# A new table of delays between the interleaved instruction streams of a hybrid decoder layer

## The chip, the cores and the metric

The kernel runs on one core of one Trainium2 chip. The metric is the time of one launch in microseconds (us). Three runs of the kernel before took 1193.43, 1197.82 and 1200.17 us, median 1197.82.

## The reference, cut to what matters

One decoder layer is applied to a prompt of 512 tokens (with 16 learned meta tokens in front) and to 8 samples of 8 new tokens each, with a cache of 2048 keys and values per sample in pages of 128.

```python
xn = rmsnorm(x, p['ln_mix_pre'])
h = xn @ p['w_in']                       # one projection for everything below
da_q, da_k, da_v, gdn_qkv, gdn_z, gdn_b, gdn_a, gate_a, gate_b = jnp.split(h, SPLIT_POINTS, axis=-1)
o_a = attn_fn(q, k, v, lam)              # differential attention: prompt (causal) or sample (paged cache)
o_a = (rmsnorm(o_a, p['da_subln']) * (1.0 - lam_init)).reshape(bsz, t, DA_V_WIDTH)
qkv, new_gdn_conv = causal_dwconv(gdn_qkv, gdn_conv_buf, p['gdn_conv_w'])
# gated DeltaNet (GDN), 4 heads: a triangular solve per chunk, then a recurrence over chunks
o_b = rmsnorm(o_b, p['gdn_norm']) * jax.nn.silu(gdn_z...)
mix = jax.nn.sigmoid(gate_a) * (o_a @ p['w_branch_a']) + jax.nn.sigmoid(gate_b) * (o_b @ p['w_branch_b'])
x = x + rmsnorm(mix @ p['w_out'], p['ln_mix_post'])
# then a gated feed-forward block with a causal convolution of width 3
up, gate = jnp.split(xn @ p['w_ffn_in'], 2, axis=-1)
x = x + rmsnorm((jax.nn.gelu(gate) * up) @ p['w_down'], p['ln_ffn_post'])
```

The outputs are the two groups' rows and the new keys, values and states.

## The kernel before, in words

Activations stand transposed, with channels on the 128 partitions and the 592 tokens (512 prompt, 64 sample, 16 meta) along the free axis. A dense product is made in two halves of the token axis, 256 and 336 columns (or 322, where most meta tokens are not needed). Each operand is split into a rounded part and a remainder (`split`), and a product is three matmuls for each 128 channels: high by high, high by low, low by high. Half a product over 1024 channels is thus a group of 24 matmuls (`dense_steps`).

The stages follow each other: embedding and queries; then a part in which two streams of work are merged; then the rest of the mix, the output projection and the feed-forward block. The change acts on the merged part alone.

The two streams are Python generators. `main` is the prompt's attention (`da_main`: a stream that makes keys and values and projects GDN head 0, merged with one that uses them, head by head), then the four GDN heads (`gdn`: the chain of one head merged with the projection and convolution of the next), then the split of the GDN output. `rest` is the sample attention in chunks of 256 keys (`sample_attention`: four pairs of samples, each of eight chunks and one for the new keys), then the sixteen products for the gates (`gate`), and then the first branch product (`branch_a`), which waits until `spare` is set, when the base inversion of the last GDN head has been emitted.

A chain of GDN (`gdn_chain`) is a row of dependent steps: decays, transposed and normalised keys, the Gram matrices, the inverse of 16x16 diagonal blocks by 14 steps on VectorE (`gdn_base`), larger blocks by TensorE (`gdn_solve`), the samples' states, then four chunks of the recurrence, then the z gate. Between steps it yields a delay out of the table, `yield DELAY[n]`: entries 1 to 5 lie before the base inversion, 12 right after it, 13 to 17 in the solve (15 is used twice), 6 to 8 in the samples' states, 9 to 11 in the recurrence, four times each. Entry 0 ends a projection. Entries 21 to 25 lie in the keys, the meta attention and the prompt attention (23 after the norm of a head's output, 24 after a block's softmax, 25 after the transposition of its weights). Entry 26 lies in each chunk of the sample attention, between the transposition of the weights and their product with the values; the loads of the chunk's value pages are emitted before it, and the next chunk's keys too.

The planner, `merge`, keeps a clock: `work`, the planned time of all matmuls emitted so far, plus `idle`. Each stream has a share, and of those that are ready the one furthest behind its share emits up to its next yield. A stream that yields a delay isn't ready until the clock has moved on by so much:

```python
n = math.prod(rhs.shape[1:])
self.work += (1.68e-3 if lhsT.dtype == F32 and lhsT.shape[1] > 32 else 0.42e-3) * n
...
if s[3] > self.work + self.idle + 1e-6:
    continue
...
s[3] = self.work + self.idle + delay
```

A transposition counts as 0.11 us. When nobody is ready, `drain` moves the clock by 0.1 us of `idle` and asks again. While the prompt attention runs, `main` has share 600 (`MAIN_1`) and `rest` has `REST_W`; in the GDN heads `main` has 1e9, so that `rest` emits only while `main` waits. A planned half group costs 24 x 256 x 0.42e-3 = 2.58 or 24 x 336 x 0.42e-3 = 3.39 us; the gates yield twice as often (steps of 1.29 and 1.62 us).

What the planner makes is the order of emission. The framework then orders each engine's instructions, taking that order for priorities, and gives out buffers: the pages of the cache have six buffers (`page`, line 1386 loads them), transposed keys four, TensorE's results in PSUM two for `d` (dense products), three for `t`, two for `g` and one for `s`. The gates' buffers take the memory of the sample attention, so that the gates' tanh (line 1587) can't run before that attention has ended. All loads are issued by SyncE's queue.

Lines that the prediction speaks of: 275 is every matmul, 423 every transposition, 317 and 318 the two parts of a split; 656 a convolution's multiply-add; 798 and 799 scale the keys; 1352 normalises attention rows; 1469 is the exponential of a chunk of the sample attention; 1587 a gate's tanh; 1603 the branch product's evacuation.

Of the kernel before, what the change touches and what calls it, by code (L numbers as in the profile page):

```python
# [52 lines left out]
def _lay_out_constants():  # L53
# [76 lines left out]


DELAY = (
    10.08, 5.4, 0.6, 0.6, 6.0, 1.3, 0.9, 0.85, 1.32, 1.0, 1.68, 0.17, 26.0, 0.67, 2.93, 0.77,
    0.09, 0.85, 0.38, 2.28, 0.05, 1.54, 0.74, 1.56, 6.12, 0.84, 1.4, 11.52, 1.4, 1.68, 10.28,
)
KEYS = 2
CHUNKS_S = PAST // 256
# [8 lines left out]
FINE = 8  # L146
MAIN_1 = 600.0
MAIN_2 = 1e9
REST_W = 165.0


class Body:
# [39 lines left out]
    def run(self):  # L192
# [14 lines left out]
        with ExitStack() as sm:  # L207
            with ExitStack() as s1:
# [3 lines left out]
                with ExitStack() as s2:  # L212
# [17 lines left out]
                    def main():  # L230
                        head = {}
                        yield from self.da_main(dpool, self.gdn_project(0, head))
                        da.close()
                        self.chain = True
                        self.psum_g = self.pool(ctx, "psum_g", space=PSUM)
                        with ExitStack() as s:
                            self.gpool = self.pool(s, "gpool")
                            yield from self.gdn(head)
                        yield from self.mix_parts(self.pool(s2, "mix"))

                    def rest():
                        with ExitStack() as s:
                            yield from self.sample_attention(self.pool(s, "sa", side="right"))
                        self.gates, self.gtpool = {}, self.pool(sm, "gates", side="right")
                        for i in range(16):
                            yield from self.gate(i)
                        while not self.spare:
                            yield None
                        yield from self.branch_a()

                    self.drain(self.merge((main(), lambda: MAIN_2 if self.chain else MAIN_1), (rest(), REST_W)))
                    self.banks = "ggsttdd"
# [2047 lines left out]
```

## Time and profile before

| what | us |
|---|---|
| median of the runs | 1197.82 |
| lowest and highest run | 1193.43, 1200.17 |
| the profiled execution's own time | 1194.08 |
| its span, from first to last instruction | 1192.2 |
| TensorE matmul busy | 1133.1 |
| VectorE busy | 741.1 |
| ScalarE busy | 554.9 |
| mean granted TensorE clock | 0.985 |

A profile is one execution. Busy time is a union over an engine's instructions; PE stands for matmuls, PEld for loads of weights beside them, DVE for VectorE, ACT for ScalarE, POOL for GpSimd, SP for SyncE, and a trailing q for an engine's instruction queue. A row of a line gives the shortest, median and longest duration in ns, and the first and the last start in us. In a table by stretches each engine has its busy us and, in brackets, its number of instructions. In a row of waits stand the us in total, the number of waits and the longest.

### The profile page before, as it was taken

What the parts mean: (1) busy time and instruction counts of PE and PEld (TensorE: products, weight loads), DVE (VectorE), ACT (ScalarE), POOL (GpSimd) and SP (SyncE); (2) the same over time, 40 slices, a digit from 0 to 9 for tenths busy, and PEclk for the clock granted to TensorE, in tenths of its full rate; (3) what the DMA queues carried; (4) which work ended last, traced back from release to release, by engine and by line L of the source; (5) the groups of instructions that cost most, each with busy time, mean ns of one, the idle gap of its engine ahead of it and who ended that gap; (6) DMA issues with size and microseconds to landing.
All of it is one profiled execution on the core that took longest, in us unless ns stands there. A gap on an engine that the chain in (4) does not pass through costs nothing. (4 is left out here: it accounts for less than half of the span.)

```text
span 1192.2 us, 23895 instructions
## 1 busy us (share of the span) xinstructions
PE 1133.1 (95%) x8683; PEld 1019.3 (85%) x8683; DVE 741.1 (62%) x2007; ACT 554.9 (47%) x1421; POOL 223.5 (19%) x348
## 2 busy tenths in 40 slices
PE   6999999989988999999998999999999999999997
PEld 5987788777657767999988787789999999999996
DVE  5447667785448535763357585479899889842323
ACT  5235444554554553433332445355555555732321
POOL 2122221130001001100010001334554544300000
PEclk9999999999999989999999999999999999999999
DMA  6357454648685863232311245233333322432322
GB/s 201 79 206 224 153 159 132 202 127 307 220 279 188 295 201 92 73 90 56 105 56 45 65 124 177 96 107 106 99 91 91 106 85 86 131 102 79 97 74 80
DMA packets 184349, 157.57 MB, mean 132 GB/s; under 512 B 12570, under 2 KB 146273, under 8 KB 184231
## 3 DMA queue, kind: packets, MB, share of 16 engines
q1 hardware_dynamic: 179713, 147.53, 40.5%
q0 software_dynamic: 3264, 5.16, 1.2%
q10 hardware_dynamic: 1254, 3.35, 0.9%
q8 instruction: 69, 1.13, 0.4%
q14 instruction: 49, 0.40, 0.1%
HBM read 146.12 MB, written 9.88 MB: 131 GB/s over the span
## 5 line engine op out<-in xcount | busy, mean ns | idle before, releaser
L318 DVE TENSOR_TENSOR wlo<-wraw,whi 128x512 fp32r<-128x512 f32 x196 | 138.4, 720 | 139.1 <-ACT whi L317 138.0
L275 PE MATMUL ps_d<-xhi,whi 128*128 128x256 f32 (+2 forms) x704 | 218.9, 311 | 0.0
L275 PE MATMUL ps_d<-xhi,wlo 128*128 128x256 f32 (+2 forms) x704 | 214.2, 305 | 1.3 <-DVE wlo L318 1.3
L275 PE MATMUL ps_d<-xlo,whi 128*128 128x256 f32 (+2 forms) x704 | 214.2, 304 | 0.3 <-DVE xlo L318 0.2
L317 ACT CAST whi<-wraw 128x512 fp32r<-128x512 f32 (+1 forms) x198 | 117.4, 610 | 176.4 <-PE ps_d L275 88.9
L275 PEld LDWEIGHTS ps_d<-xhi,whi 128*128 128x128 f32 x704 | 135.2, 192 | 5.1 <-issue 3.1
L275 PEld LDWEIGHTS ps_d<-xlo,whi 128*128 128x128 f32 x704 | 135.2, 192 | 3.9 <-issue 2.6
L275 PEld LDWEIGHTS ps_d<-xhi,wlo 128*128 128x128 f32 x704 | 134.8, 192 | 4.0 <-DVE wlo L318 2.0
L1421 ACT COPY KT<-ps_t 128x512 f32<-128x512 f32 x107 | 59.1, 588 | 41.6 <-PE ps_t L423 41.4
L423 PE MATMUL ps_t<-consts,page 128*128 128x128 f32 x512 | 73.6, 286 | 2.7 <-DVE o L1480 2.6
L423 PEld LDWEIGHTS ps_t<-consts,page 128*128 128x128 f32 x512 | 60.0, 147 | 15.9 <-PE ps_t L275 5.7
L275 PE MATMUL ps_t<-fhit,hw 128*128 128x290 f32 x228 | 68.0, 298 | 0.0
L275 PE MATMUL ps_t<-flot,hw 128*128 128x290 f32 x228 | 67.7, 297 | 0.0
L275 PE MATMUL ps_t<-fhit,lw 128*128 128x290 f32 x228 | 67.6, 297 | 0.0
L317 ACT CAST hw<-sw 128x512 fp32r<-128x512 f32 x76 | 47.2, 622 | 41.4 <-PE ps_g L275 20.1
L318 DVE TENSOR_TENSOR lw<-sw,hw 128x512 fp32r<-128x512 f32 x76 | 60.2, 792 | 6.4 <-ACT hw L317 6.3
L275 PE MATMUL ps_s<-KT,qb 128*32 128x256 f32 x512 | 44.0, 392 | 3.3 <-DVE xc L974 1.8
L275 PEld LDWEIGHTS ps_t<-flot,hw 128*128 128x128 f32 x228 | 43.3, 190 | 0.0
L275 PEld LDWEIGHTS ps_t<-fhit,lw 128*128 128x128 f32 x228 | 43.1, 189 | 0.0
L275 PEld LDWEIGHTS ps_t<-fhit,hw 128*128 128x128 f32 x228 | 43.0, 189 | 0.0
L275 PE MATMUL ps_t<-page,pT 128*32 128x256 f32 x512 | 38.5, 410 | 0.9 <-ACT pT L1432 0.9
L1978 DVE SCALAR_TENSOR_TENSOR fy<-fpre,fw,fy 128x592 f32<-128x592 f32 x44 | 36.5, 831 | 1.0 <-ACT fy L1976 0.2
(700 smaller groups left out, 3076.7 us busy)
## 6 DMA issues: line engine op xcount, KB each, us to landing
page<-in_cache_k SPq DMA_DIRECT2D x128, 256.0 KB, 3.3
page<-in_cache_v SPq DMA_DIRECT2D x128, 256.0 KB, 4.5
wraw<-in_w_in SPq DMA_DIRECT2D x88, 256.0 KB, 3.3
wraw<-in_w_ffn_in SPq DMA_DIRECT2D x50, 256.0 KB, 3.2
wraw<-in_w_down SPq DMA_DIRECT2D x40, 256.0 KB, 3.1
raw<-in_w_ffn_in SPq DMA_DIRECT2D x38, 256.0 KB, 2.8
wraw<-in_w_out SPq DMA_DIRECT2D x16, 256.0 KB, 2.9
x<-in_x_prompt SPq DMA_DIRECT2D x4, 512.0 KB, 8.8
```

Source lines behind the costliest of these rows:

```text
L275: return self.nc.tensor.matmul(out, lhsT, rhs, **kw).ins
L317: self.nc.scalar.copy(hi, raw)
L318: (eng or self.nc.vector).tensor_tensor(out=lo, in0=raw, in1=hi.bitcast(F32), op=ALU.subtract)
L423: self.nc.tensor.transpose(out, in_, self.ident[:k, :k])
L1421: copy(kt[:, :, 128 * j : 128 * j + 128], tp)
L1978: nc.vector.scalar_tensor_tensor(out=y, in0=pre[:, j : j + 592], scalar=fw[:, m, 16 + j : 17 + j], in1=y, op0=ALU.mult, op1=ALU.add)
```

## The change

24 of the 31 entries of the table of delays get new values, and the share of the second stream goes from 165.0 to 168.5. The code that uses them is untouched.

```diff
 DELAY = (
-    10.08, 5.4, 0.6, 0.6, 6.0, 1.3, 0.9, 0.85, 1.32, 1.0, 1.68, 0.17, 26.0, 0.67, 2.93, 0.77,
-    0.09, 0.85, 0.38, 2.28, 0.05, 1.54, 0.74, 1.56, 6.12, 0.84, 1.4, 11.52, 1.4, 1.68, 10.28,
+    9.27, 2.17, 0.6, 0.6, 1.61, 1.42, 3.06, 2.05, 0.23, 1.0, 3.15, 0.12, 25.87, 1.27, 2.93, 1.46,
+    0.06, 0.16, 0.13, 2.31, 0.54, 1.29, 0.49, 6.72, 6.58, 0.14, 3.65, 11.52, 1.4, 1.3, 10.28,
 )
...
-REST_W = 165.0
+REST_W = 168.5
```

Entry by entry, old to new: 0: 10.08 to 9.27; 1: 5.4 to 2.17; 4: 6.0 to 1.61; 5: 1.3 to 1.42; 6: 0.9 to 3.06; 7: 0.85 to 2.05; 8: 1.32 to 0.23; 10: 1.68 to 3.15; 11: 0.17 to 0.12; 12: 26.0 to 25.87; 13: 0.67 to 1.27; 15: 0.77 to 1.46; 16: 0.09 to 0.06; 17: 0.85 to 0.16; 18, 19 and 20: 0.38, 2.28, 0.05 to 0.13, 2.31, 0.54; 21: 1.54 to 1.29; 22: 0.74 to 0.49; 23: 1.56 to 6.72; 24: 6.12 to 6.58; 25: 0.84 to 0.14; 26: 1.4 to 3.65; 29: 1.68 to 1.3.

## The prediction

> **What bounds the kernel now.** I read the page first (span, engines, slices), then busy time by stage, then the stretches in which TensorE stood idle.
>
> ```profile
> span 1192.2 us, 23895 instructions
> PE 1133.1 (95%) x8683; PEld 1019.3 (85%) x8683; DVE 741.1 (62%) x2007; ACT 554.9 (47%) x1421; POOL 223.5 (19%) x348
> PEclk9999999999999989999999999999999999999999
> ```
>
> TensorE is busy for 95% of the span, so work is conserved and only the other 59 us, and time at a lower granted clock, can be won. The change can act only while the streams are merged. The stage table gives that part (columns: stretch in us, its length, busy us and instruction count of PE, PEld, DVE, ACT, POOL, then granted clock, DMA share, GB/s):
>
> ```profile
> 52.00:240.00 188.00, 183.17 (x1495) 151.58 (x1495) 120.16 (x468) 89.15 (x268) 43.29 (x87) 0.99 0.55 172
> 240.00:357.00 117.00, 106.47 (x1006) 79.90 (x1005) 67.42 (x254) 64.61 (x191) 12.78 (x22) 0.97 0.72 235
> 357.00:460.00 103.00, 94.78 (x850) 72.63 (x850) 59.78 (x218) 51.34 (x159) 8.55 (x20) 0.93 0.67 219
> 460.00:618.00 158.00, 156.88 (x1173) 152.55 (x1173) 81.68 (x233) 59.08 (x169) 11.68 (x18) 1.00 0.28 74
> 618.00:690.00 72.00, 64.33 (x435) 57.27 (x434) 48.48 (x153) 23.40 (x69) 5.02 (x5) 0.95 0.18 53
> ```
>
> The stretches are prompt attention (52 to 240) and then the four GDN heads. Idle PE is length less busy: 4.8, 10.5, 8.2, 1.1 and 7.7 us, together 32.3. Clock lost is length times (1 - clock): 3.5 us in the first head, 7.2 in the second, 3.6 in the last. What sets the stretches apart is the filler beside the chain. The rows of the sample attention's exponential (by source line, asked for each head), of the gates' tanh and of the branch product show which filler ran when (the last two numbers of each are first and last start):
>
> ```profile
> L1469 ACT ACTIVATE S<-S,nm x14: 342/509/513, 264.3 to 353.9; 128x256 f32<-128x256 f32 x13, 128x64 f32<-128x64 f32 x1
> L1469 ACT ACTIVATE S<-S,nm x11: 337/509/513, 386.4 to 449.5; 128x256 f32<-128x256 f32 x9, 128x64 f32<-128x64 f32 x2
> L1587 ACT ACTIVATE gt<-ps_d x32: 380/409/457, 459.9 to 618.2; 128x256 f32<-128x256 f32 x16, 128x322 f32<-128x322 f32 x16
> L1603 DVE SCALAR_TENSOR_TENSOR gt<-gt,ps_d x16: 410/450/492, 631.4 to 669.0; 128x256 f32<-128x256 f32 x8, 128x322 f32<-128x322 f32 x8
> ```
>
> So heads 0 and 1 are filled with 14 and 11 chunks of sample attention, head 2 with gates, head 3 with the branch product alone. Beside gates PE idles 1.1 us in 158; beside chunks 18.7 in 220. Per chunk the loss is (18.7 + 3.5 + 7.2) / 25 = 1.2 us. And between the last gate (618.2) and the first branch product (631.4) filler is missing, which the timeline of PE shows (start, length, what, idle before it and its releaser):
>
> ```profile
> 620.11 0.39 PE L275 MATMUL ps_d<-vt,whi 128*128 128x256 f32 x1 [0.60 <-DVE vt L318]
> ...
> 622.67 0.26 PE L423 MATMUL ps_t<-consts,kn 80*128 80x80 f32 x1 [1.35 <-DVE kn L798]
> ...
> 627.89 0.53 PE L275 MATMUL ps_d<-q,whi 128*128 128x256 f32 x2 [0.62 <-ACT q L317]
> ...
> 630.60 0.57 PE L275 MATMUL ps_d<-qb,whi 128*128 128x256 f32 x1 [2.18 <-DVE qb L318]
> ```
>
> One more reading decides how much a delay can do. The gates' tanh starts at 459.9, yet matmuls of the first gate (322 columns; the z gate has that width too, but its first half is evacuated only at 469.5, first row) lie among the chunks of head 1:
>
> ```profile
> L714 ACT ACTIVATE z<-ps_d x2: 385/410/436, 469.5 to 474.8; 128x256 f32<-128x256 f32 x1, 128x322 f32<-128x322 f32 x1
> ...
> 407.93 0.39 PE L275 MATMUL ps_d<-xhi,wlo 128*128 128x322 f32 x1
> 408.16 0.31 PE L275 MATMUL ps_d<-xhi,whi 128*128 128x322 f32 x1
> ...
> 412.19 0.60 PE L423 MATMUL ps_t<-consts,page 128*128 128x128 f32 x4
> 412.54 0.39 PE L275 MATMUL ps_d<-xhi,whi 128*128 128x322 f32 x1
> ```
>
> The code emits a half group in one piece, and page transposes stand inside one here. So the order of emission is a priority and not the order on PE: a step emitted before its inputs are ready doesn't block PE, and one emitted late can still be pulled up. Delays decide who goes first among what is ready. That makes all terms small.
>
> **The change, part by part.** No instruction, DMA or byte is added or removed; the table moves whole steps against each other. Costs come from the profiled execution (1194.1 us, span 1192.2), 3.7 below the median of the runs, 1197.8.
>
> *Entries without effect: 0.* Numbers 18 to 20 and 29 are never reached (the tail solve returns before its first wait; 27 to 30 are not read). Entry 22 is one wait in the meta attention, shorter by 0.25: 0.
>
> *The share of the second stream, 165 to 168.5.* It gets 2% more of about 45 us of planned work up to 240, a quarter of a chunk: 0, because the chunk runs in one place or the other.
>
> *Prompt attention: entries 21, 23, 24, 25.* Entry 23 (after the norm of a head's output, once per head) goes from 1.56 to 6.72, the others by +0.46, -0.70 and -0.25. PE did wait at that spot:
>
> ```profile
> PE ps_t L423 <- DVE on L1352: 3.0, 3, 1.3
> ```
>
> The gain is at most these 3.0 us. The loss: 4 x 5.16 = 21 us of planned waiting, filled by keys, projections and chunks; only the last head has little of them, so one wait, 5 us, bounds it. With PE busy 183.2 of 188 I take -1 (the row of the idle time lies nearer than a bare wait). Ends -3 and +5.
>
> *Head of the GDN chain: entries 1, 4, 5 and 12.* Per head 5.4 + 6.0 + 1.3 + 26.0 = 38.7 becomes 2.17 + 1.61 + 1.42 + 25.87 = 31.1. The chain asks for its steps 7.6 us sooner, and the next head's projection (17.9 planned) is then not wholly in front of the base inversion. VectorE has to do convolution and inversion side by side: it is busy 16.85 of 19 us in 262 to 281 even now. What is late next is the projection's convolution, which only the next head needs. I take 0. The rows for both (that stretch, a convolution's multiply-add by its line, PE's waits for the scaled keys):
>
> ```profile
> 262.00:281.00 19.00, 16.58 (x168) 12.01 (x168) 16.85 (x92) 9.08 (x26) 1.12 (x3) 0.91 0.81 273
> ...
> L656 DVE SCALAR_TENSOR_TENSOR cy<-pre,cw,cy x36: 836/846/862, 185.7 to 504.5; 128x616 f32<-128x616 f32 x36
> ...
> PE ps_t L423 <- DVE kn L798: 2.5, 2, 1.4
> ```
>
> Ends: -4 (the 2.4 us that PE idles in that first stretch and the 1.7 us of clock lost there) and +8 (the three multiply-adds of one convolution, 0.85 us each, in front of the inversion in heads 0 to 2, 7.6 us). What PE waited for the scaled keys, 2.5 us, can grow or shrink within these.
>
> *Solve, tail and recurrence: entries 6, 7, 8, 10, 11, 13, 15, 16, 17.* Solve 9.01 to 10.27 (15 is used twice), tail 3.07 to 5.34, recurrence 4 x 2.85 = 11.4 to 4 x 4.27 = 17.1: together +9.2. Beside gates a delay is rounded up to gate steps of 1.3 or 1.6 planned us; about two more steps per head come out. In heads 1 and 2 PE has work for them. In head 3 filler is short at the end: +1, ends 0 and +4.
>
> *The chunk's own wait: entry 26, 1.4 to 3.65.* A chunk is planned as 16 + 2 transposes of 0.11 and 16 products of 0.107, that is 3.70 us. When nothing else is ready, the planner lets the wait run idle, and this idle time counts against the chain's delays too. A chunk alone then uses up 5.10 us of chain delays before and 7.35 after. With the sums above (chain 63.4 to 65.0 per head, less 17.9 for the projection) chunks per head fall to (47.1 / 7.35) / (45.5 / 5.10) = 0.72 of what they were: from 14 to about 10 in head 0, and some 8 in head 1. Seven chunks are left for head 2, and eight or nine gates (7 x 7.35 / 5.83) move from head 2 to head 3. What this saves:
> - Head 3 has gates beside its beginning, and the branch product is emitted later. The four gaps above (4.8 us) go, and the clock there (3.6 us lost in that stretch) half comes back. Late next is the second of the two, the chain's own 0.7 us steps on VectorE, so I take -5; ends -8 and 0.
> - Heads 0 to 2 have the same 25 chunks over about 45 us more. If the loss per chunk stays 1.2 us, nothing is won; if it goes with density, a quarter of 29 us goes. I take -4; ends -12 and +8 (seven chunks, now in a head where the loss was nearly nil, bring 1.2 us each).
>
> On the clock: a 6.5 us stretch of head 1, PE busy for all but 0.2 us of it and most of that small products and transposes, was granted 0.81.
>
> ```profile
> 415.00:421.50 6.50, 6.33 (x48) 4.25 (x45) 0.49 (x2) 2.10 (x6) 0.00 (x0) 0.81 0.68 245
> ```
>
> The Trainium skill (TensorE: Matmul & The Clock Gate, Part 4) says that transposes do not count as PE activity for the clock gate. The stretch agrees with it; by that rule the clock lost would follow the number of transposes, which stays, and the forecast would be some 2 us higher.
>
> The sum: -1 + 0 + 1 - 5 - 4 = -9 us. On the profiled 1194.1 this gives 1185; on the median of the runs 1189. The forecast is **1188 us**, between the two and nearer to the median.
>
> **Rivals.** About 6 us, 0.5%, is what a measurement of this kernel can tell from no change.
>
> *Nothing to tell.* Order on PE is set by readiness, as the gate matmuls at 408 show, and the two tables then give nearly the same program. Against it: gates did stay out of head 3, and chunks out of head 2. Time 1192 to 1204, centre 1198. Chance 0.20.
>
> *Slower: the chunk's value pages are held longer.* The loads of a chunk's value pages are emitted ahead of the lengthened wait, and the products that free them after it. All pages share six buffers and a chunk takes four, so each chunk may hold up the next one's loads by 3.65 - 1.4 = 2.25 us. For it speaks that the load queue waits just there in heads 0 and 1 (waits of the DMA queue, 240 to 460):
>
> ```profile
> SPq L1386 <- PE ps_t L275: 45.6, 19, 6.4
> SPq L1386 <- PE ps_t L423: 26.3, 24, 11.0
> ...
> page<-in_cache_v SPq DMA_DIRECT2D x128, 256.0 KB, 4.5
> ```
>
> The first row is loads waiting for the value product. Against it: a value page takes 4.5 us from issue to landing (last row, DMA issues), so part of the longer wait has to pass anyway, and PE pulls up other work. If ten of the 25 chunks pay in full, it costs 22.5 us and the sum is +13: 1211. It decides against the forecast from four paying chunks on. Chance 0.30, by itself or with convolution in the way of the inversion.
>
> *Much faster.* Filler lasts to the end of the chain, and the loss per chunk halves: -5 - 12, and 3 more from the stretch to 690: 1178 to 1170, centre 1174. Against it: by my count 88 planned us of delays in head 3 (60 gate steps of 1.46) still meet only 8 or 9 gates and the branch product, about 73. Chance 0.10.
>
> **How the numbers follow.** Forecast (1178 to 1191) 0.40, much faster 0.10, nothing to tell 0.20, slower 0.30. Faster by over 0.5% is the first two, 0.50; the likeliest single case is the forecast, and its own range is 1178 to 1191. The range leaves out the far parts of the outer cases: 1168 to 1214, from the ends of the chunk and head-3 terms below to the priced slower rival above.
>
> **What would show it.** In the profile of the changed kernel: exponentials of chunks still after 460 and the first gate tanh well after 480; the last gate tanh after 640; no PE gap over 1 us between last gate and first branch product; a granted clock in heads 0 and 1 above 0.95. If the loss per chunk is the same, idle time appears beside chunks in head 2 instead. If the value pages are held, the load queue's waits for the value product grow beyond 45.6 us. The prediction is wrong if chunks end at 450 as before (the wait was filled anyhow), or if PE idles beside the inversions with VectorE full.

## The result, and the profile after

| what | before | after |
|---|---|---|
| median of the runs | 1195.81 us (beside the runs of after) | 1156.80 us (1156.19 to 1157.30) |
| ratio, 95% interval | | 0.967 (0.9637 to 0.9702) |
| span of the profiled execution | 1192.2 us | 1154.8 us |

The new table is faster by 3.3%, 39 us, where 10 us were forecast. It lies below the whole range. The direction was right and so was the place, the part where the streams are merged; the size was not.

The page of after (its span, engines, and the clock by slices):

```profile
span 1154.8 us, 23883 instructions
PE 1113.5 (96%) x8683; PEld 1009.6 (87%) x8683; DVE 738.9 (64%) x2007; ACT 553.4 (48%) x1421; POOL 219.6 (19%) x348
PEclk9999999999999999999999999999999999999999
```

The same 8683 matmuls are busy for 20 us less (1133.1 before), and the slice of the clock that stood at 8 is gone. Busy time hides the clock: in these traces products of 256 columns start 120 ns apart at full clock and 213 ns apart at half clock, transposes 109 and 213.

The merged part ends where the rest of the mix begins (the first evacuation of the second branch product), at 689.2 before and at 651.3 after. The next rows give the merged part and what follows, columns as in the stage table of the prediction. Before:

```profile
52.00:689.20 637.20, 604.82 (x4946) 513.13 (x4946) 376.72 (x1321) 287.17 (x852) 81.32 (x150) 0.98 0.49 153
689.20:1192.20 503.00, 486.98 (x3458) 469.04 (x3456) 339.25 (x615) 246.03 (x526) 134.70 (x179) 0.99 0.34 102
```

After:

```profile
52.00:651.30 599.30, 585.30 (x4946) 503.62 (x4946) 373.21 (x1320) 284.72 (x851) 80.16 (x150) 1.00 0.52 162
651.30:1154.80 503.50, 487.08 (x3458) 469.10 (x3457) 340.65 (x617) 246.84 (x527) 131.88 (x179) 0.99 0.35 103
```

The rest is the same, 503.0 and 503.5 us, and the whole gain, 637.2 - 599.3 = 37.9 us, lies in the merged part, with 4946 matmuls in both. It has three parts. Idle PE falls from 637.20 - 604.82 = 32.4 to 14.0 us, by 18.4. Time at half clock falls from nine windows of 3.41 us (30.7 us) to one (3.4 us); by the spacings above nearly half of each is lost, so that is at most 13.7. The other 5.8 us, at least, are busy time at full clock.

Where PE idled: each head has a beginning (from the start of its chain to the end of the base inversion) and a rest. In heads 0 and 1 of before these are the two rests:

```profile
280.00:357.00 77.00, 70.22 (x681) 50.95 (x680) 31.78 (x111) 42.83 (x123) 3.81 (x7) 0.98 0.81 265
402.00:477.00 75.00, 70.85 (x613) 54.40 (x613) 30.76 (x100) 35.63 (x105) 4.20 (x7) 0.93 0.57 189
```

And all eight stretches of after, beginning and rest by turns:

```profile
240.00:275.00 35.00, 33.44 (x304) 26.92 (x302) 31.18 (x136) 19.41 (x59) 7.25 (x15) 1.00 0.63 204
275.00:325.00 50.00, 49.18 (x483) 37.25 (x483) 24.94 (x85) 28.58 (x87) 3.72 (x6) 1.00 0.69 224
325.00:364.00 39.00, 35.59 (x318) 30.95 (x316) 35.49 (x140) 19.85 (x65) 7.05 (x14) 1.00 0.68 221
364.00:419.00 55.00, 53.43 (x521) 40.14 (x521) 27.03 (x89) 31.69 (x95) 3.21 (x6) 1.00 0.72 235
419.00:461.00 42.00, 39.63 (x343) 33.68 (x343) 36.05 (x140) 21.50 (x69) 6.73 (x11) 1.00 0.70 221
461.00:520.00 59.00, 57.97 (x476) 52.06 (x477) 26.75 (x72) 24.04 (x72) 3.64 (x6) 1.00 0.35 97
520.00:553.00 33.00, 31.36 (x238) 30.56 (x238) 26.44 (x102) 14.13 (x44) 2.90 (x2) 1.00 0.26 63
553.00:647.00 94.00, 94.00 (x718) 92.30 (x718) 35.01 (x75) 29.55 (x74) 2.71 (x3) 1.00 0.27 74
```

The rests of heads 0 and 1 idle 0.8 and 1.6 us instead of 6.8 and 4.2, the last head's rest not at all, and every stretch has the full clock. Over four heads, beginnings idle 9.0 us (14.0 before) and rests 3.4 (13.0 before).

Which filler ran when (rows of the chunks' exponential asked for heads 0, 1 and 2, the gates' tanh, and the first row of the branch product's evacuation):

```profile
L1469 ACT ACTIVATE S<-S,nm x10: 361/509/541, 256.5 to 323.3; 128x256 f32<-128x256 f32 x9, 128x64 f32<-128x64 f32 x1
L1469 ACT ACTIVATE S<-S,nm x10: 348/510/529, 353.3 to 416.4; 128x256 f32<-128x256 f32 x9, 128x64 f32<-128x64 f32 x1
L1469 ACT ACTIVATE S<-S,nm x5: 350/508/512, 451.1 to 470.9; 128x256 f32<-128x256 f32 x4, 128x64 f32<-128x64 f32 x1
L1587 ACT ACTIVATE gt<-ps_d x32: 383/408/448, 482.4 to 610.9; 128x256 f32<-128x256 f32 x16, 128x322 f32<-128x322 f32 x16
L1603 DVE SCALAR_TENSOR_TENSOR gt<-gt,ps_d x20: 412/450/492, 614.2 to 675.0; 128x256 f32<-128x256 f32 x10, 128x322 f32<-128x322 f32 x10
```

Heads 0 to 2 have 10, 10 and 5 chunks where they had 14, 11 and 0. The last chain ends at 647. Of the 20 evacuations in the last row the first 16 belong to the first branch product, and the last of these starts at 650.3: filler lasts to the end. Chains are shorter too; they end at 325, 419, 520 and 647 (357, 477, 608 and 684 before).

### The profile page after: what moved, and what is told of

Its sections match the earlier page's. It is cut to its first block, busy times and chain, and to the rows that moved or that the text cites. A ratio compares the mean times of both kernels' runs of the same rounds, so it can differ in the third digit from the quotient of the medians.

```text
span 1154.8 us, 23883 instructions
## 1 busy us (share of the span) xinstructions
PE 1113.5 (96%) x8683; PEld 1009.6 (87%) x8683; DVE 738.9 (64%) x2007; ACT 553.4 (48%) x1421; POOL 219.6 (19%) x348
## 4 chain that ended last, share of the span: by engine, by line
PE 78%; issue 9%; DVE 6%; ACT 2%; POOL 2%; DMA 1%; SPq 0%; DVEq 0%; POOLq 0%; ACTq 0%
PE ps_d L275 29%; PE ps_t L275 21%; PE ps_g L275 15%; PE ps_t L423 7%; PE ps_s L275 5%; PE ps_m L275 1%; POOL grr L387 1%; ACT KT L1421 1%; DVE cy L656 1%; DVE wlo L318 0%; DVE row L978 0%; DVE xc L980 0%; DMA page<-in_cache_v 0%; DVE row L979 0%; DMA x<-in_x_prompt 0%
## 5 line engine op out<-in xcount | busy, mean ns | idle before, releaser
L423 PE MATMUL ps_t<-consts,page 128*128 128x128 f32 x512 | 69.4, 277 | 0.4 <-ACT KT L1421 0.3
L423 PEld LDWEIGHTS ps_t<-consts,page 128*128 128x128 f32 x512 | 56.9, 141 | 12.7 <-issue 5.1
L275 PE MATMUL ps_t<-page,pT 128*32 128x256 f32 x512 | 36.0, 384 | 0.0
```

The costliest lines, as they stand in the source:

```text
L275: return self.nc.tensor.matmul(out, lhsT, rhs, **kw).ins
L423: self.nc.tensor.transpose(out, in_, self.ident[:k, :k])
```

## Experiments

Each is a change of the order of work alone. Ratios are to the kernel before, run on the same chip beside them. "Chunks" are the numbers of chunks' exponentials in the prompt part (up to 240) and in heads 0, 1, 2; "idle" and "half clock" are PE's idle time and the time at half clock in the merged part.

### Single groups of the table, on the old table

The chunk's wait alone:

```diff
-    0.09, 0.85, 0.38, 2.28, 0.05, 1.54, 0.74, 1.56, 6.12, 0.84, 1.4, 11.52, 1.4, 1.68, 10.28,
+    0.09, 0.85, 0.38, 2.28, 0.05, 1.54, 0.74, 1.56, 6.12, 0.84, 3.65, 11.52, 1.4, 1.68, 10.28,
```

> Entry 26 alone goes from 1.4 to 3.65. Theory A (the filler is spread out: fewer chunks in heads 0 and 1, gates left for head 3) puts most of the gain here: 1160 to 1175, with exponentials of chunks after 460 and gates' tanh up to 600 or later. Theory B (the chain's own delays, entries 1 to 17, now fit its steps) expects 1188 to 1198. Theory C (prompt attention and the second stream's share) expects 1193 to 1198.

Measured: 1171.1 us, ratio 0.9809 (0.9788 to 0.9831), -24 us. Chunks 10, 9, 9, 8; idle 16.4, half clock 6.8 us. So one number carries most of it, as theory A expected. The last chain ends at 635 and filler is left over, which then runs alone:

```profile
635.00:664.00 29.00, 29.00 (x219) 29.00 (x218) 16.79 (x32) 7.19 (x14) 0.00 (x0) 1.00 0.28 83
```

PE isn't idle there, but 29 us of dense products lie behind the chain that could have lain beside it.

The head of the GDN chain (entries 1, 4, 5, 12) alone:

```diff
-    10.08, 5.4, 0.6, 0.6, 6.0, 1.3, 0.9, 0.85, 1.32, 1.0, 1.68, 0.17, 26.0, 0.67, 2.93, 0.77,
+    10.08, 2.17, 0.6, 0.6, 1.61, 1.42, 0.9, 0.85, 1.32, 1.0, 1.68, 0.17, 25.87, 0.67, 2.93, 0.77,
```

> Entries 1, 4, 5 and 12 alone (the chain's steps up to the base inversion asked for 7.6 us sooner per head). Theory A expects 1190 to 1200. Theory B expects 1165 to 1185, with heads that begin their inversion 5 us or more sooner. Theory C expects 1193 to 1198.

Measured: 1188.43, 0.9946 (0.9926 to 0.9966), -6.5 us; chunks 11, 12, 13, 0, idle 32.4, half clock 23.9. None of the three theories gave this time. Idle time is that of before (32.4 us); what fell is the time at half clock, by 6.8 us.

Solve, tail and recurrence (entries 6, 7, 8, 10, 11, 13, 15 to 17) alone:

```diff
-    10.08, 5.4, 0.6, 0.6, 6.0, 1.3, 0.9, 0.85, 1.32, 1.0, 1.68, 0.17, 26.0, 0.67, 2.93, 0.77,
-    0.09, 0.85, 0.38, 2.28, 0.05, 1.54, 0.74, 1.56, 6.12, 0.84, 1.4, 11.52, 1.4, 1.68, 10.28,
+    10.08, 5.4, 0.6, 0.6, 6.0, 1.3, 3.06, 2.05, 0.23, 1.0, 3.15, 0.12, 26.0, 1.27, 2.93, 1.46,
+    0.06, 0.16, 0.38, 2.28, 0.05, 1.54, 0.74, 1.56, 6.12, 0.84, 1.4, 11.52, 1.4, 1.68, 10.28,
```

> Entries 6, 7, 8, 10, 11, 13, 15, 16 and 17 alone (solve, samples' states and recurrence wait 9.2 us longer per head). Theory A expects 1195 to 1205, since chains grow longer and filler runs out sooner. Theory B expects 1175 to 1190. Theory C expects 1193 to 1198.

Measured: 1208.51, 1.0125 (1.0094 to 1.0155), +13.6 us; chunks 11, 16, 9, 0, idle 39.3, half clock 42.9; slower than even theory A expected. Head 0 has 16 chunks instead of 14: longer chain delays beside a short chunk wait crowd them there.

The prompt's entries (0 and 21 to 25, with the share 168.5) alone:

```diff
-    10.08, 5.4, 0.6, 0.6, 6.0, 1.3, 0.9, 0.85, 1.32, 1.0, 1.68, 0.17, 26.0, 0.67, 2.93, 0.77,
-    0.09, 0.85, 0.38, 2.28, 0.05, 1.54, 0.74, 1.56, 6.12, 0.84, 1.4, 11.52, 1.4, 1.68, 10.28,
+    9.27, 5.4, 0.6, 0.6, 6.0, 1.3, 0.9, 0.85, 1.32, 1.0, 1.68, 0.17, 26.0, 0.67, 2.93, 0.77,
+    0.09, 0.85, 0.38, 2.28, 0.05, 1.29, 0.49, 6.72, 6.58, 0.14, 1.4, 11.52, 1.4, 1.68, 10.28,
-REST_W = 165.0
+REST_W = 168.5
```

> Entries 0, 21, 22, 23, 24, 25 and the second stream's share alone on the old table. Taken back from the new table they cost 12.5 us. If they act by themselves: 1180 to 1186. If they act only where the chunks are spread out: 1191 to 1198.

Measured: 1189.55, 0.9963 (0.9936 to 0.9991), -5.3 us, between the two ranges. The four groups alone give -24 - 6.5 + 13.6 - 5.3 = -22; together they give -39.

### Groups taken back from the new table

The chunk's wait taken back to 1.4:

```diff
-    0.06, 0.16, 0.13, 2.31, 0.54, 1.29, 0.49, 6.72, 6.58, 0.14, 3.65, 11.52, 1.4, 1.3, 10.28,
+    0.06, 0.16, 0.13, 2.31, 0.54, 1.29, 0.49, 6.72, 6.58, 0.14, 1.4, 11.52, 1.4, 1.3, 10.28,
```

> The new table with entry 26 back at 1.4. Theory A expects most of the gain gone: 1180 to 1196, gates ended before head 3 begins. Theory B and theory C expect 1157 to 1165.

Measured: 1201.11, 1.0061 (1.0039 to 1.0083). Chunks 12, 15, 9, 0; idle 36.1, half clock 27.3. Without entry 26 all the other edits together make the kernel 0.6% slower, more than theory A expected; in their company it is worth 44 us.

Solve, tail and recurrence taken back:

```diff
-    9.27, 2.17, 0.6, 0.6, 1.61, 1.42, 3.06, 2.05, 0.23, 1.0, 3.15, 0.12, 25.87, 1.27, 2.93, 1.46,
-    0.06, 0.16, 0.13, 2.31, 0.54, 1.29, 0.49, 6.72, 6.58, 0.14, 3.65, 11.52, 1.4, 1.3, 10.28,
+    9.27, 2.17, 0.6, 0.6, 1.61, 1.42, 0.9, 0.85, 1.32, 1.0, 1.68, 0.17, 25.87, 0.67, 2.93, 0.77,
+    0.09, 0.85, 0.13, 2.31, 0.54, 1.29, 0.49, 6.72, 6.58, 0.14, 3.65, 11.52, 1.4, 1.3, 10.28,
```

> The new table with the old values of entries 6, 7, 8, 10, 11, 13, 15, 16 and 17. These cost 13.6 us alone on the old table, since they pack more filler into each head. If they cost the same beside entry 26: 1140 to 1148, faster than the new table. Theory D: they are the counterweight to entry 26 and the time is 1158 to 1170, with filler left over after the last chain as with entry 26 alone.

Measured: 1164.27, 0.9747 (0.9725 to 0.977), 7.5 us above the new table. So this group costs 13.6 us alone and saves 7.5 beside the long chunk wait: its sign depends on entry 26. Without it the last chain ends at 615 and the leftover runs alone for longer:

```profile
615.00:659.00 44.00, 44.00 (x330) 44.00 (x329) 18.60 (x34) 10.46 (x22) 0.00 (x0) 1.00 0.27 77
```

Idle time is as in after (14.2 us), so the loss is mostly busy time at full clock. What makes it is only argued. The chunks' products of 32 columns run four at a time, started 7 ns apart (the 512 with the keys, 382 ns each, are busy for 45.0 us in the page of after). At full clock, two such groups start 196 ns apart; from the last of them to other work it is 310 ns, and the first of them starts some 90 ns late behind other work. So a run broken off by other work costs about 0.2 us. There are 56 unbroken runs of such products in after and 69 here, which would make some 3 us. Over the 20 traces of this case, busy time at full clock goes with the number of runs (correlation 0.8), but before has 56 too and at least 5.8 us more than after, so this isn't all of it.

The prompt's edits taken back:

```diff
-    9.27, 2.17, 0.6, 0.6, 1.61, 1.42, 3.06, 2.05, 0.23, 1.0, 3.15, 0.12, 25.87, 1.27, 2.93, 1.46,
-    0.06, 0.16, 0.13, 2.31, 0.54, 1.29, 0.49, 6.72, 6.58, 0.14, 3.65, 11.52, 1.4, 1.3, 10.28,
+    10.08, 2.17, 0.6, 0.6, 1.61, 1.42, 3.06, 2.05, 0.23, 1.0, 3.15, 0.12, 25.87, 1.27, 2.93, 1.46,
+    0.06, 0.16, 0.13, 2.31, 0.54, 1.54, 0.74, 1.56, 6.12, 0.84, 3.65, 11.52, 1.4, 1.3, 10.28,
-REST_W = 168.5
+REST_W = 165.0
```

> The new table with the old values of entries 0, 21, 22, 23, 24, 25 and of the second stream's share. Theory C (prompt attention matters by itself): 1162 to 1172. The others expect 1155 to 1161.

Measured: 1169.35, 0.978 (0.9755 to 0.9805): the prompt's edits are worth 12.5 us in company. Idle 19.8, half clock 13.7. The stage up to 240 in this run and in after, in this order:

```profile
52.00:240.00 188.00, 182.11 (x1486) 153.07 (x1485) 123.86 (x479) 94.08 (x285) 44.95 (x90) 0.99 0.53 167
```

```profile
52.00:240.00 188.00, 186.39 (x1527) 155.53 (x1527) 126.03 (x481) 93.59 (x283) 42.96 (x87) 0.99 0.56 176
```

So 5.9 - 1.6 = 4.3 us of it are idle time in the prompt, with 41 more matmuls done by 240. Another 5.2 us at most are clock, and this lies far behind: without the prompt's edits the half clock stands from 489.6 to 499.8, in head 2.

The chunk's wait and the chain's head, on the old table:

```diff
-    10.08, 5.4, 0.6, 0.6, 6.0, 1.3, 0.9, 0.85, 1.32, 1.0, 1.68, 0.17, 26.0, 0.67, 2.93, 0.77,
-    0.09, 0.85, 0.38, 2.28, 0.05, 1.54, 0.74, 1.56, 6.12, 0.84, 1.4, 11.52, 1.4, 1.68, 10.28,
+    10.08, 2.17, 0.6, 0.6, 1.61, 1.42, 0.9, 0.85, 1.32, 1.0, 1.68, 0.17, 25.87, 0.67, 2.93, 0.77,
+    0.09, 0.85, 0.38, 2.28, 0.05, 1.54, 0.74, 1.56, 6.12, 0.84, 3.65, 11.52, 1.4, 1.68, 10.28,
```

> Entry 26 and entries 1, 4, 5 and 12 new, the rest old. Entry 26 alone gave 1171, the chain's head alone 1188 (from 1195). If the two add: 1164 to 1166. If the other chain entries are needed beside entry 26 (theory D, chain delays and chunk wait fit each other): 1166 or more.

Measured: 1171.73, 0.9809 (0.9787 to 0.9831), chain's end at 615. The head's 6.5 us are not had on top of the wait.

### Which property of the chunk's wait does it

The longer wait does two things. It uses up planner time, so that fewer chunks fit beside a chain (this the prediction counted), and it keeps the chunk's stream standing between transposing the weights and multiplying by the values. The first without the second: the clock is charged, the wait stays 1.4 (the table's entry 26 is 1.4 in this and the next two).

```diff
+            self.idle += 2.25
             yield DELAY[26]
```

> The new table with entry 26 at 1.4, but at the same place the planner's clock is moved on by 2.25 us at once: the chunk is charged as before the change plus 2.25, and its own stream waits no longer than 1.4. Theory A1 (what counts is that chunks use up more of the chain's delays, so that chains are emitted sooner and filler lasts): 1155 to 1172, heads ending within some 15 us of the new table's. Theory A2 (what counts is that the chunk's value product is asked for later, after its pages and weights are there): 1185 to 1203, near the 1201 of the run with entry 26 at 1.4.

Measured: 1186.64, 0.9934 (0.9911 to 0.9957). Chunks 11, 11, 12, 2: it doesn't spread as far, so a larger charge followed:

```diff
+            self.idle += 3.0
             yield DELAY[26]
```

> The new table with entry 26 at 1.4 and the planner's clock moved on by 3.0 us per chunk. In the order of emission and of TensorE this spreads the chunks as the new table does: before the first, second and third head's state step stand 16, 11 and 9 of them (new table 16, 10, 10; entry 26 at 1.4 alone 20, 14, 2; charge 2.25: 17, 12, 7). Theory A1 (the spreading of chunks is what counts): 1155 to 1168. Theory A2 (the wait inside the chunk counts by itself): 1178 or more, close to the 1187 of the charge of 2.25.

Measured: 1198.72, 1.0028 (1.0005 to 1.0052). Chunks 10, 11, 11, 4, nearly the spreading of after, and no gain at all. The rows show where the time is, first three heads' beginnings and then the rest of head 0:

```profile
240.00:277.00 37.00, 31.53 (x274) 24.18 (x273) 30.21 (x131) 15.08 (x42) 5.59 (x12) 0.91 0.58 178
336.00:384.00 48.00, 42.04 (x356) 35.75 (x353) 36.89 (x140) 22.56 (x70) 8.99 (x15) 0.93 0.54 172
447.00:498.00 51.00, 43.84 (x359) 37.44 (x359) 38.27 (x149) 22.23 (x71) 8.38 (x12) 0.90 0.50 152
277.00:336.00 59.00, 57.72 (x557) 43.01 (x556) 27.90 (x95) 33.17 (x99) 3.84 (x7) 1.00 0.80 256
```

The rest of head 0 is as good as in after (1.3 us idle). The beginnings idle 5.5, 6.0 and 7.2 us where after idles 1.6, 3.4 and 2.4, and each is at 0.90 to 0.93 of the clock. In head 1, PE waits there for the squares of the chain's queries (line 777 on ScalarE) and then for the rounded weights of the next head's projection (`whi`, `wlo`), with nothing beside it (start, length, what, idle before and its releaser):

```profile
340.04 0.33 PE L423 MATMUL ps_t<-consts,q 128*128 128x128 f32 x1 [2.12 <-ACT gjunk L777]
...
343.70 0.58 PE L275 MATMUL ps_d<-xhi,whi 128*128 128x256 f32 x1 [1.76 <-ACT whi L317]
346.18 0.58 PE L275 MATMUL ps_d<-xhi,wlo 128*128 128x256 f32 x1 [1.12 <-DVE wlo L318]
```

In after the projection's products already stand among the transposes of the queries at that place:

```profile
329.76 0.33 PE L423 MATMUL ps_t<-consts,q 128*128 128x128 f32 x1
329.86 0.39 PE L275 MATMUL ps_d<-xhi,whi 128*128 128x336 f32 x1
```

ScalarE's times show the difference: in after it rounds the first of these weights at 323.9, before the queries' squares (327.8 to 330.1), and in this run at 343.0, behind them (339.6 to 342.0). Head 2 is the same: 417.1 before 421.8, and here 454.7 behind 453.6. So the projection, which is filler for the chain's preparation, comes too late here. Whether the order of emission alone puts it there no run shows.

So the spreading of chunks, brought about in this way, is no gain by itself. The opposite test keeps the stream's wait of 3.65 and sets the clock back, so that the wait uses up no more than before:

```diff
             yield DELAY[26]
+            self.idle -= 2.25
```

(entry 26 at 3.65.)

> The new table with entry 26 at 3.65, and after the wait the planner's clock is set back by 2.25 us, so that chains don't get that time for nothing. Chunks before the state steps are 21, 13 and 2, as crowded as with entry 26 at 1.4 (20, 14, 2), but each chunk's value product is asked for 3.65 us after its weights. Theory A1: 1190 to 1205, near the 1201 of entry 26 at 1.4. Theory A2: 1155 to 1175.

Measured: 1204.97, 1.0093 (1.0062 to 1.0123); chunks 12, 15, 9, 0. The wait without spreading is no use either: in these runs it takes both. Both edits also act on the chains (the charge releases their steps all at once, the clock set back holds them longer), and no run separates that from the rest.

The same total wait in another place, 2.25 of it behind the chunk and 1.4 where it was:

```diff
                 if before["c"] == CHUNKS_S:
                     divide(before)
-            yield 0.0
+            yield 2.25
```

> The new table with the chunk's 3.65 us of waiting cut in two: 1.4 before the value product (as in the old table) and 2.25 after the chunk's last step. Chunks before the state steps: 16, 11, 9. Theory A1' (the chunk's stream must stand still for 3.65 us of planner time in all, so that chains and their filler alternate; where is indifferent): 1155 to 1168. Theory A2' (the longer wait has to lie in front of the value product): 1178 to 1200.

Measured: 1174.45, 0.9842 (0.9815 to 0.9869). Chunks 11, 10, 10, 5, exactly those of after. The next rows are the rest of head 0 and the beginning of head 1:

```profile
280.00:330.00 50.00, 49.55 (x496) 37.96 (x496) 24.91 (x85) 30.06 (x89) 3.73 (x6) 1.00 0.79 255
330.00:377.00 47.00, 42.01 (x346) 36.16 (x342) 37.28 (x142) 22.73 (x70) 7.11 (x15) 0.93 0.55 177
```

The rest of the head is as full as in after; the beginning idles 5.0 us (3.4 in after), and there too the projection's weights are rounded at 336.3, behind the queries' squares (332.2 to 335.3). Over four heads, beginnings idle 15.1 us and rests 5.5. The time lies between the two ranges. From 1201 (entry at 1.4) to 1174, 27 us, it is the stream's standing still and the spreading that comes with it, wherever the stop stands. From 1174 to 1157, some 18 us, the chunks are spread alike and only the place of the stop differs. Why a stop before the value product brings the projection earlier is not settled.

### The size of the wait, and two neighbours

Entry 26 at other values in the new table; the line is changed in that number alone:

```diff
-    0.06, 0.16, 0.13, 2.31, 0.54, 1.29, 0.49, 6.72, 6.58, 0.14, 3.65, 11.52, 1.4, 1.3, 10.28,
+    0.06, 0.16, 0.13, 2.31, 0.54, 1.29, 0.49, 6.72, 6.58, 0.14, 2.5, 11.52, 1.4, 1.3, 10.28,
```

> The new table with entry 26 at 2.5; chunks before the state steps 18, 12, 6. If the time follows the spreading smoothly: about half way from 1201 (1.4) to 1157 (3.65), 1175 to 1185. If the order of instructions behaves by chance, anything from 1160 to 1205.

> The new table with entry 26 at 3.4; chunks before the state steps 17, 10, 9. Smooth: 1157 to 1163. By chance: 10 us or more away from 1157.

> The new table with entry 26 at 3.9; chunks before the state steps 16, 10, 9 and 1 in the last head. Smooth: 1156 to 1163 (5.0 gave 1182). By chance: 10 us or more away from 1157.

> The new table with entry 26 at 5.0. Chunks before the state steps: 15, 8, 9 and 4 in the last head. If chunks beside chains always cost by their density, 1150 to 1157. If a balance is met at 3.65 (filler ends with the last chain there, gates and chunks left over afterwards here), 1158 to 1175, as with the chain's other entries old.

| entry 26 | time, us | ratio, 95% interval | chunks | idle / half clock, us |
|---|---|---|---|---|
| 1.4 | 1201.11 | 1.0061 (1.0039 to 1.0083) | 12, 15, 9, 0 | 36.1 / 27.3 |
| 2.5 | 1185.16 | 0.9925 (0.9901 to 0.995) | 11, 12, 13, 0 | 28.5 / 19.5 |
| 3.4 | 1164.89 | 0.975 (0.9725 to 0.9775) | 11, 10, 10, 5 | 16.8 / 10.2 |
| 3.65 | 1156.80 | 0.967 (0.9637 to 0.9702) | 11, 10, 10, 5 | 14.0 / 3.4 |
| 3.9 | 1169.87 | 0.9793 (0.9769 to 0.9817) | 11, 9, 10, 6 | 17.7 / 17.1 |
| 5.0 | 1182.33 | 0.9914 (0.9886 to 0.9943) | 10, 9, 8, 9 | 25.0 / 10.2 |

A valley about 3.65; neither expectation for 5.0 came true, and 3.9 is 13 us above the new table, as "by chance" had it. Between 3.4 and 3.65 the spreading is the same, and 8 us lie between them: that much can be the accident of one order. So a difference of 10 us between two runs says little about a cause.

Two small steps away from the new table, the wait of the base inversion back to 26.0, and a larger share of the second stream:

```diff
-    9.27, 2.17, 0.6, 0.6, 1.61, 1.42, 3.06, 2.05, 0.23, 1.0, 3.15, 0.12, 25.87, 1.27, 2.93, 1.46,
+    9.27, 2.17, 0.6, 0.6, 1.61, 1.42, 3.06, 2.05, 0.23, 1.0, 3.15, 0.12, 26.0, 1.27, 2.93, 1.46,
```

> The new table with entry 12 back at 26.0 from 25.87, the smallest step of the change: the chunks stand as in the new table (16, 10, 10), some matmuls trade places. If the last ten us of the gain are one order among neighbours (3.4 gave 1165, 3.9 gave 1170): 1160 to 1170. If the time depends on the spreading alone: 1155 to 1159.

```diff
-REST_W = 168.5
+REST_W = 185.0
```

> The new table with the second stream's share at 185 instead of 168.5: about one more chunk beside prompt attention, where PE idles less than beside the heads' beginnings (chunks before the state steps 17, 10, 9). If a chunk moved there saves its loss of about 1.2 us: 1154 to 1157, faster than the new table. If the order of neighbours decides: 1160 to 1172.

Measured: 1158.05, 0.971 (0.9686 to 0.9734), which isn't told apart from the new table; and 1166.12, 0.9781 (0.9756 to 0.9806), some 9 us more. None of the runs beats the new table.

## Why the prediction was wrong

**What held.** The arithmetic of the planner's clock: 10, then some 8, then seven chunks were forecast for heads 0 to 2; 10, 10 and 5 came. The planned delays per head add up to the 63.4 and 65.0 us of the prediction with entry 14 counted twice, like 15. Chunks' exponentials run after 460 (last at 470.9), the first gate's tanh is at 482.4, and PE has no gap over 1 us between the last gate and the first branch product. Heads 0 and 1 have the full clock. One sign did not come: the last gate's tanh is at 610.9 and not after 640, since the chains end earlier too. The slower rival did not come: the load queue's wait for the value product (second row), 45.6 us before, did not grow; the wait for the keys' and weights' transposes (first row) did, from 26.3, and the two together stayed, 71.9 and 69.8 (waits of that queue in after, 240 to 471):

```profile
SPq L1386 <- PE ps_t L423: 35.2, 18, 11.6
SPq L1386 <- PE ps_t L275: 34.6, 15, 7.2
```

**The step that failed: the spreading of the chunks, -4 with ends -12 and +8.** It reckoned with a loss per chunk of 1.2 us, of which at most a quarter, the change in density, would go. In after, heads 0 to 2 idle 1.6 + 0.8 + 3.4 + 1.6 + 2.4 + 1.0 = 10.8 us beside 25 chunks and lose no clock: 0.43 us per chunk, so that 29.4 - 10.8 = 18.6 us went where 4 were forecast and 12 was the most. Two things were missed. The loss wasn't tied to the chunk as such: the same chunks, spread nearly alike, lose much or little with where the stream stands still (1157, 1174 and 1199 us for the wait before the value product, the wait behind the chunk and the charge of 3.0). The likely reason, argued and not shown, is that a stream that stops in the middle of a chunk has products to give PE later, when the chain stands still. And 10.7 of the 29.4 us were clock, which was counted as if it went with the chunks; it went with idle time (below), and both fell together.

**The last head, -5 with ends -8 and 0.** Too small by the same reckoning. Idle time from 460 to 690 was 1.1 + 7.7 us and the clock lost 3.6, together 12.4; in after the last head idles 1.6 us, all in its beginning, so 10.8 us went where 5 were forecast. The argument against filler lasting to the chain's end (88 planned us of delays against 73 of filler) was wrong: the chain ended at 647, the branch products at 650. So the "much faster" rival had the right mechanism, and its halved loss per chunk was still too little.

**The prompt, -1 with ends -3 and +5.** Alone the group gives -5.3 us, in company -12.5. The 3.0 us that PE waited for the head's norm were taken for the upper bound, but the stage idled 4.8 us in all and now idles 1.6. In company up to 5.2 us more are clock in head 2, which the term didn't look at; how the prompt's order reaches that far stays open.

**Solve, tail and recurrence, +1.** +13.6 alone, -7.5 in company: no term of a sum at all. **Chain head, 0 with ends -4 and +8:** -6.5 alone, nothing on top of the chunk's wait. **The share of the second stream, 0:** 165 to 168.5 wasn't run by itself; another step of that number, to 185, costs 9 us, so that "the chunk runs in one place or the other" was no reason for zero. The sum over single entries was thus wrong in form: the edits act on each other. That they balance, chain delays against chunk waits, so that filler and chain end together, fits the runs (filler is left over for 29 us with entry 26 alone and for 44 with solve, tail and recurrence taken back).

**Work is conserved.** This premise put a term at nothing: at least 5.8 us of the gain are busy time at full clock. Over the 20 traces nearly the same matmuls of the merged part take from 584 to 596 us at full clock (busy time less half of what lies at half clock), by order alone. The broken runs of 32-column products explain a part at most; the rest stays open.

**The clock.** The prediction saw in the stretch at 415 an agreement with the rule that transposes lower the clock. Pairs of neighbouring windows of before speak against it (columns as above; what counts is PE busy of 3.41 us in the one and the granted clock in the next):

```profile
340.52:343.93 3.41, 1.25 (x13) 0.98 (x10) 2.89 (x9) 1.81 (x6) 0.00 (x0) 1.00 0.81 236
343.93:347.35 3.42, 3.01 (x18) 2.08 (x22) 0.93 (x3) 2.83 (x7) 0.00 (x0) 0.50 0.84 295
384.90:388.31 3.41, 1.20 (x26) 0.71 (x30) 3.41 (x19) 1.60 (x8) 0.00 (x0) 1.00 0.46 144
388.31:391.72 3.41, 3.41 (x26) 2.40 (x19) 3.06 (x15) 1.36 (x4) 0.00 (x0) 0.50 0.49 147
...
429.27:432.68 3.41, 2.39 (x32) 1.76 (x28) 1.61 (x6) 1.01 (x5) 0.00 (x0) 1.00 0.77 282
432.68:436.09 3.41, 3.41 (x27) 2.07 (x20) 0.48 (x1) 0.92 (x3) 0.00 (x0) 0.50 0.54 171
627.24:630.65 3.41, 0.61 (x4) 0.35 (x3) 3.41 (x9) 0.60 (x1) 0.00 (x0) 1.00 0.00 0
630.65:634.07 3.42, 3.42 (x14) 3.04 (x15) 2.77 (x12) 0.62 (x1) 0.00 (x0) 0.50 0.00 0
```

Three of the four windows in front were idle for 63, 65 and 82%, the one at 429 for 30%. In the merged part of five traces (before, after, entry 26 at 1.4, solve and tail alone, charge of 2.25), cut into windows of 3.413 us along the edges of the clock's records, all 21 windows at full clock with at least half their time idle were followed by half clock, 4 of 10 with 40 to 50% idle, and 4 of 849 with less. In 61 windows idle time and transposes together take 60% or more (idle time alone under 40%), and none of them was followed by half clock. The Trainium skill (TensorE: Matmul & The Clock Gate, Part 4) says that a transpose isn't counted as busy in the way that a matmul is; these 61 windows do not agree, and the 2 us that the prediction gave to that rule were not there. The time at half clock in the merged part fell from 30.7 to 3.4 us with the same transposes. In the window of the prediction's stretch, 415.6 to 419.0, transposes take 17%. It is one of the four exceptions; these spent half of their time or more in small matmuls of the chain and the prompt (4 to 64 columns), and why these lower the clock stays open.

## What to carry to other kernels

When two streams are merged by a table of delays, the time that one stream stands still is a size to be set, like a tile. Set it together with the delays of the stream beside it, since the effects of single entries add up neither in size (-22 for the parts, -39 for the whole) nor in sign (+13.6 for solve, tail and recurrence alone, -7.5 in company). Look for the stretches in which PE idles 1.7 us or more within 3.4 us: each was paid for twice here, once as idle time and once in nearly half of the next window. And compare where the chain ends with where the filler ends: filler left over behind the chain could have lain beside it. Last, try neighbours of a table before explaining it: here 8 us lie between two waits of 3.4 and 3.65 with the same spreading.

## What was not expected of the hardware

The clock falls on short gaps. In the kernel before, this one gap (timeline of PE, start, length, what, idle before it) was all the idle time in the window from 340.52 to 343.93:

```profile
343.81 1.47 PE L423 MATMUL ps_t<-consts,page 128*128 128x128 f32 x6 [2.16 <-DVE o L1480]
```

It was enough to halve the granted clock for the next 3.41 us. The Trainium skill (the same page, Part 1) gives a free-running window of about 3.4 us and a clock of either half or full; the rows agree with both (in before, all edges of the half-clock stretches of the merged part lie whole multiples of 3.413 us apart). Its practical rule there, no idle gaps over some 3.4 us, is too lax for this trace: what counted was the share of a window, from about a half on.
